# RWKV7 in two blocks of 16: substitution for 16-blocks, the step to 32 on TensorE, and low halves on VectorE

## The chip, the cores and the metric

The kernel runs on one core of one Trainium2 chip. The time is device microseconds of one execution; the metric is the median of the runs. The engines are PE (TensorE), PEld (its weight load), DVE (VectorE), ACT (ScalarE), POOL (GpSimd) and SP (SyncE, which here issues most DMAs). Every engine works off its own list of instructions in order and waits for the others through semaphores.

## The reference

Two transformer blocks on 512 context tokens and further latent ones, width 1024, fp32. The first has a gated linear recurrence and dilated attention, the second a pooling, differential attention, RWKV7 in both directions, and a mixture of experts. The change lies in the RWKV7. Per head it carries a 64x64 state over the tokens, which each token decays, partly erases along one key and updates along another:

```
S_t = S_{t-1} * w_t  +  (S_{t-1} a_t) b_t^T  +  v_t k_t^T
y_t = S_t r_t
```

The kernel takes 64 tokens (a chunk) at once. Within a chunk the erasing terms hang on each other: they are a triangular system (I - A) X = R with a 64x64 strictly triangular A for each head and chunk, whose inverse T is wanted.

## The kernel before

A scheduler decides the order on each engine while the kernel is built, from the program's order and its own estimates; so an engine's list mixes the recurrence with the projections and the attention around it. The weights of projections come in fp32 and are split in `split_chunk` into a high half `wh` (ScalarE, L304) and a low half `wl` (GpSimd, L305), each 128x1024 per piece; a projection is three matmuls into `pf` or `pt` (L310 to L312).

The recurrence goes in 12 batches, two directions taking turns, each of two chunks with eight heads: 16 systems of 64x64, or on 128 partitions. A batch has three parts.

- `ph_a` (from L1128) loads `kb` and `kr` on SP, scans the decays (`cs`, L1142 and L1144), forms `BK` (L1156) and `AR`, multiplies them on TensorE (`pA`, L1162) and writes the masked product to `AMB` (VectorE, L1166); `ptb` (L1171) transposes.
- `ph_i` (L1178) inverts the 32x32 blocks on the diagonal. Four DMAs write them to `atD` in DRAM (L1183) and one reads them back as `LT` (L1186), with each system on a partition, repeated four times, so that each partition has eight of the 32 columns. Then come 31 steps of substitution on VectorE, each a product into `Tm` (L1194) and a sum into `Ti` (L1196), 62 instructions of 28 to 76 elements a partition. Four DMAs write `Ti` to `ttD` (L1199).
- `ph_b` (L1201) runs two batches later. It loads the inverse blocks as `TT` (four DMAs, L1213) and makes the block off the diagonal of the 64x64 inverse with three groups of 16 matmuls of 32x32 into `pi` (L1250, L1255, L1260), each copied out half by VectorE and half by ScalarE (L1245, L1246). Then `px` (L1268), its copy `XV` (L1271, L1272), `pW` (L1282), `WW` (L1289 to L1292), the outputs and the new state `SI` (L1300 to L1312).

`pW` of a batch needs `XV`, and what follows it needs `WW`; both come from VectorE and ScalarE. VectorE's list has these between the steps of another batch's substitution.

Of the kernel before, what the change touches and what calls it, by code (L numbers as in the profile page):

```python
# [39 lines left out]
def _consts():  # L40
    f = np.float32
    groups, off = {g: [] for g in "012345"}, {}
    where = {"bias1": "1", "invf": "1", "cos2": "3", "sin2": "3", "hsel": "5", "hbc": "5",
             "mask": "2", "tinit": "2", "sgn": "2",
             "iota32": "4", "tokid": "4", "tri": "4", "slot": "4", "tokrow": "4"}
# [48 lines left out]
    sg = np.ones((128, 2))  # L94
    for dd, (lt, le) in enumerate(((r[:, None] < r[None, :], r[:, None] <= r[None, :]),
                                   (r[:, None] > r[None, :], r[:, None] >= r[None, :]))):
        tr = np.concatenate([lt, le], 1)
        for e in range(2):
            m[64 * e:64 * e + 64, dd, e] = -0.5 * tr
            m[64 - 64 * e:128 - 64 * e, dd, e] = tr  # L100
    for e in range(2):
        sg[64 * e:64 * e + 64, e] = -0.5
    add("mask", m)
    add("sgn", sg)
    ti = np.zeros((4, 32, 8, 32))
    for g in range(4):
        for q in range(8):
            ti[g, :, q, 4 * q + g] = 1
    add("tinit", ti)
    return {"cst" + g: np.concatenate(v, 1) for g, v in groups.items()}, off  # L110


# [78 lines left out]
def _build(ctx, tc, A, out, dbg, upto):  # L191
# [7 lines left out]
    cur = {}  # L199
# [100 lines left out]
    def split_chunk(raw, name="w"):  # L300
# [1 line left out]
        hi = cur["wp"].tile([128, kt, nw], F32R, tag="hi", name=name + "h", bufs=cur["wb"])  # L302
        lo = cur["wp"].tile([128, kt, nw], F32R, tag="lo", name=name + "l", bufs=cur["wb"])
        SC.activation(hi, raw, AF.Copy)  # L304
        GP.tensor_tensor(lo, raw, hi.bitcast(F32), ALU.subtract)  # L305
        return hi, lo

    def mm3(p, ah, al, bh, bl, start, stop):
# [789 lines left out]
    ones64 = cc("ones")[:, 0:1].to_broadcast([128, 64])
    CW = 0.5 * math.exp(-0.5)
    atD = [dp.tile([2, 2, 8, 32, 32], F32, name="atD%d" % i) for i in range(4)]  # L1100
    ttD = [dp.tile([2, 2, 8, 32, 32], F32, name="ttD%d" % i) for i in range(4)]
    yD = [dp.tile([128, 8, 4, 64], F32, name="yD%d" % d) for d in range(2)]
    par = ((0, E0), (1, E1))
    WWB = 1
    LATB, LPN = 10, (6, 5, 5, 3)

    def w1(name, shape=(4, 64), bufs=1, dt=F32):
# [12 lines left out]
    for d in range(2):  # L1120
        for e in range(2):
# [2 lines left out]
            ir = slice(64, 128) if e == 0 else slice(0, 64)  # L1124
            V.tensor_copy(t[ir], bc(ident[ir, None, ir], [64, 4, 64]))
            SI[d, e] = t

    def ph_a(d, c, s, AMB):  # L1128

# [45 lines left out]
                          AF.Copy, scale=sgn[:, e:e + 1])  # L1175
        return AR, dec

    def ph_i(d, AMB, bi):  # L1178

        for e in range(2):  # L1180
            for i in range(2):
                r0 = 64 * e + 32 * i
                SY.dma_start(atD[bi][e, i].rearrange("q s t -> s q t"),  # L1183
                             AMB[r0:r0 + 32, e, :, :, 32 * i:32 * i + 32].rearrange("p s f t -> p (s f) t"))
        LT = w1("LT", (32, 32), 2)
        SY.dma_start(LT.rearrange("p s t -> p (s t)"),  # L1186
                     atD[bi].rearrange("e i q s t -> (e i q) (s t)")[None].to_broadcast([4, 32, 1024]))
# [9 lines left out]
        td = ttD[bi].rearrange("e i q (j g) t -> g (e i q) j t", g=4)  # L1197
        for g in range(4):
            SY.dma_start(td[g], T[32 * g:32 * g + 32])  # L1199

    def ph_b(d, chs, sts, AMB, bi):  # L1201

        lat, c0 = chs[0] >= 4, min(chs)
        XE, XO = XV1 if lat and d else XV
        T = TT[d]
        fs = [(s, f) for s in range(2) for f in range(4)]
        v3 = vTD[:, c0:c0 + 2].rearrange("t c (f e v) -> e t (c f) v", f=4, e=2)
        SY.dma_start(XE[E1, :, :, 64:128].rearrange("p s f t -> p (s f) t"), v3[0])
        SY.dma_start(XO[E0, :, :, 0:64].rearrange("p s f t -> p (s f) t"), v3[1])
        for e in range(2):  # L1210
            for i in range(2):
                r0 = 64 * e + 32 * i
                SY.dma_start(T[r0:r0 + 32, :, :, 32 * i:32 * i + 32].rearrange("p s f t -> p (s f) t"),  # L1213
                             ttD[bi][e, i].rearrange("q j t -> j q t"))

        def col(p, q, n, o=0):
            return p[:, o + n * q:o + n * (q + 1)]
# [104 lines left out]
    def run_b():  # L1322
        n, sts = pend.pop(0)
        ph_b(*sts)
        if n == 3 and dbg is not None and "S_c" in dbg:
            for d_ in range(2):
                for e, rows in par:
                    SY.dma_start(dbg["S_c"][128 * d_:128 * d_ + 128][rows, 256 * e:256 * e + 256],
                                 SI[d_, e][rows].rearrange("p a b -> p (a b)"))

    def batch(n):
        d, chs = batches[n]
        AMB = w1("AMB", (2, 2, 4, 192), 3)
# [796 lines left out]
```

## Time and profile before

| | |
| --- | --- |
| median of 3 runs | 1983.2 us (1969.72 to 1985.23) |
| the profiled execution | 1981.57 us, span 1979.7 us |
| mean granted TensorE clock over the span | 0.934 |
| PE, PEld busy | 1755.4 us (89%), 1246.3 us (63%) |
| DVE busy | 1091.5 us (55%), 2364 instructions |
| ACT, POOL busy | 619.1 us (31%), 526.5 us (27%) |

The profile is one execution taken by the hardware profiler. The first block ends near 515 us of the span; the twelve batches, with projections between, lie from there to about 1165; differential attention and merges follow, and from about 1474 us on the experts, whose weights fill the DMA queues. The granted clock is that of TensorE as a share of its full speed; matmuls are pipelined, so a busy PE need not be at its peak.

### The profile page before, as it was taken

The numbers are of one execution on the slowest core, as the hardware profiler recorded it, in microseconds if no ns is written. First come the engines' busy times: TensorE is split into PE (matmuls) and PEld (weight loads), VectorE is DVE, ScalarE is ACT, GpSimd is POOL, SyncE is SP. The second block draws the span as 40 slices with busy tenths as digits, with TensorE's granted clock in tenths as the row PEclk, the third lists the DMA queues.
The fourth block names the chain that finished last, engine by engine and source line by source line (L and its number), as shares of the span: only waits on it lengthen the run. The fifth ranks groups of instructions, "written<-read, shape, count | busy, mean of one in ns | idle before, by whom it ended". The sixth has DMA issues, their size and how long they took to land. (4 is left out here: it accounts for less than half of the span.)

```text
span 1979.7 us, 31352 instructions
## 1 busy us (share of the span) xinstructions
PE 1755.4 (89%) x12309; PEld 1246.3 (63%) x12310; DVE 1091.5 (55%) x2364; ACT 619.1 (31%) x1164; POOL 526.5 (27%) x379
## 2 busy tenths in 40 slices
PE   6899998967787887888879998988979999999998
PEld 3874677953565776677667876677954545444544
DVE  4555675275487746777788655776342333332332
ACT  4234454443443222223333233443221111111110
POOL 2510337442335332231331132642310110101010
PEclk8999998988898898889898999999979999999999
DMA  8336513567546445445355338653629999999998
GB/s 298 108 111 218 197 64 103 195 181 250 156 121 171 135 137 122 109 109 137 99 151 152 81 112 280 204 179 111 246 99 387 387 386 386 386 387 386 386 386 289
DMA packets 275295, 415.89 MB, mean 210 GB/s; under 512 B 104876, under 2 KB 126408, under 8 KB 274888
## 3 DMA queue, kind: packets, MB, share of 16 engines
q1 hardware_dynamic: 246248, 383.44, 58.0%
q10 hardware_dynamic: 25568, 16.78, 2.8%
q0 software_dynamic: 3328, 13.63, 2.4%
q8 instruction: 98, 1.61, 0.3%
q14 instruction: 53, 0.43, 0.1%
HBM read 370.26 MB, written 43.53 MB: 209 GB/s over the span
## 5 line engine op out<-in xcount | busy, mean ns | idle before, releaser
L305 POOL TENSOR_TENSOR wl<-wr,wh 128x1024 fp32r<-128x1024 f32 x125 | 308.3, 2473 | 495.8 <-ACT wh L304 455.5
L304 ACT ACTIVATE wh<-wr 128x1024 fp32r<-128x1024 f32 x125 | 131.6, 1054 | 141.2 <-issue 54.9
L1980 POOL TENSOR_TENSOR yl<-ey,yh 128x512 fp32r<-128x512 f32 x30 | 38.4, 1279 | 466.1 <-ACT yh L1979 466.1
L310 PE MATMUL pf<-h2h,wh 128*128 128x512 f32 x344 | 147.8, 430 | 15.6 <-DVE Ti L1196 10.2
L1194 DVE TENSOR_TENSOR Tm<-LT,Ti 128x60 f32<-128x60 f32 (+24 forms) x372 | 116.8, 314 | 76.9 <-DMA LT<-atD 68.2
L311 PE MATMUL pf<-h2l,wh 128*128 128x512 f32 x344 | 144.5, 420 | 0.0
L312 PE MATMUL pf<-h2h,wl 128*128 128x512 f32 x344 | 143.3, 417 | 0.0
L1974 PE MATMUL ped<-wd,hid 128*64 128x512 f32 (+1 forms) x528 | 127.5, 585 | 0.7 <-ACT hid L1958 0.7
L1935 PE MATMUL peg<-wg,hTg 128*64 128x512 f32 x512 | 126.9, 597 | 0.0
L1942 PE MATMUL peu<-wu,hTg 128*64 128x512 f32 x512 | 125.3, 595 | 0.0
L1196 DVE TENSOR_TENSOR Ti<-Ti,Tm 128x60 f32<-128x60 f32 (+24 forms) x372 | 109.3, 294 | 9.1
L2007 DVE TENSOR_TENSOR acc<-acc,pcb 128x512 f32<-128x512 f32 (+1 forms) x124 | 76.0, 665 | 49.1 <-PE pcb L2006 49.0
L310 PEld LDWEIGHTS pf<-h2h,wh 128*128 128x128 f32 x344 | 69.4, 202 | 38.4 <-issue 15.4
L1974 PEld LDWEIGHTS ped<-wd,hid 128*64 128x64 f32 x528 | 39.9, 136 | 70.6 <-issue 65.9
L1942 PEld LDWEIGHTS peu<-wu,hTg 128*64 128x64 f32 x512 | 43.2, 137 | 65.1 <-issue 62.9
L311 PEld LDWEIGHTS pf<-h2l,wh 128*128 128x128 f32 x344 | 68.8, 200 | 18.5 <-issue 3.4
L1935 PEld LDWEIGHTS peg<-wg,hTg 128*64 128x64 f32 x512 | 41.9, 137 | 60.9 <-issue 58.1
L312 PEld LDWEIGHTS pf<-h2h,wl 128*128 128x128 f32 x344 | 68.6, 199 | 18.2 <-issue 2.1
L1282 PE MATMUL pW<-AMB,XV 128*128 128x64 f32 (+1 forms) x256 | 45.2, 335 | 28.7 <-DVE XV L1271 16.9
L1979 ACT ACTIVATE yh<-ey 128x512 fp32r<-128x512 f32 x30 | 18.9, 630 | 163.6 <-DVE ey L1978 90.2
L1915 DVE TENSOR_SCALAR hTg<-pg,gs,sh 128x128 f32<-128x128 f32 x64 | 25.3, 408 | 75.1 <-PE peu L1942 38.4
L1912 ACT ACTIVATE hTg<-pg,sh,gs 128x128 f32<-128x128 f32 x64 | 28.2, 457 | 121.4 <-PE peu L1942 55.4
(961 smaller groups left out, 4475.1 us busy)
## 6 DMA issues: line engine op xcount, KB each, us to landing
wg<-in_w_exp_gate_dram SPq DMA_DIRECT2D x64, 1024.0 KB
wu<-in_w_exp_up_dram SPq DMA_DIRECT2D x64, 1024.0 KB
wd<-in_w_exp_down_dram SPq DMA_DIRECT2D x62, 1024.0 KB
wr<-in_w_in_dram SPq DMA_DIRECT2D x97, 512.0 KB
kb<-kbD SPq DMA_DIRECT2D x24, 384.0 KB
wr<-in_w_out_dram SPq DMA_DIRECT2D x16, 512.0 KB
LT<-atD SPq DMA_DIRECT2D x12, 512.0 KB
thD<-mth ACTq DMA_DIRECT2D x24, 256.0 KB
```

The costliest lines, as they stand in the source:

```text
L304: SC.activation(hi, raw, AF.Copy)
L305: GP.tensor_tensor(lo, raw, hi.bitcast(F32), ALU.subtract)
L310: PE.matmul(p, ah, bh, start=start, stop=False)
L311: PE.matmul(p, ah, bl, start=False, stop=False)
L312: PE.matmul(p, al, bh, start=False, stop=stop)
L1194: V.tensor_tensor(tmp[:, :nj, :n], bc(LT[:, s, None, ts_], [128, nj, n]), bc(T[:, js, s:s + 1], [128, nj, n]), ALU.mult)
L1196: V.tensor_tensor(T[:, js, ts_], T[:, js, ts_], tmp[:, :nj, :n], ALU.add)
L1282: PE.matmul(pw[e][:, nw * f:nw * (f + 1)], X[:, s, f, :], AMB[:, e, s, f, n0:192], start=True, stop=True)
L1935: mm = PE.matmul(pg[64 * a:64 * a + 64, :], hT[:, k, 64 * a:64 * a + 64], gp[a][k // 4][:, k % 4, :], start=(k == 0), stop=(k == 7), tile_ ...
L1942: PE.matmul(pu[64 * a:64 * a + 64, :], hT[:, k, 64 * a:64 * a + 64], up[a][k // 4][:, k % 4, :], start=(k == 0), stop=(k == 7), tile_posit ...
L1974: PE.matmul(pd[64 * a:64 * a + 64, :], hid[:, m * k + 64 * a:m * k + 64 * a + 64], dn[q][a][:, k, 0:q1 - q0], start=(k == 0), stop=(k == 3 ...
L2007: V.tensor_tensor(acc[i][:, qs], acc[i][:, qs], p, ALU.add)
```

## The change

The substitution now inverts 16x16 blocks: `atD` and `ttD` hold blocks of 16, `LT` is 128x256 (128 KB, 512 KB before) and repeated twice, and there are 15 steps (30 instructions). `Ti` is written with two DMAs, and eight read it back into a tile `U` (three buffers), which holds the 16-blocks on the diagonal of each 32-block. A new part `ph_m` joins two blocks of 16 to one of 32, with a batch between: 32 small matmuls transpose `U` (into `tit`, copied to `T16` by ScalarE), 32 multiply with `AMB`, VectorE masks that into `PJ`, 64 more give the joined block and its transpose (`tiu`), and five VectorE sums put them into `TT` and `T16`. With that `ph_b` loses its first group of 16 matmuls and its copy. `WW` gets a second buffer. And in this stage the low halves `wl` of the weights are made on VectorE: 53 of the 125.

```diff
@@ split_chunk
-        GP.tensor_tensor(lo, raw, hi.bitcast(F32), ALU.subtract)
+        cur.get("lo", GP).tensor_tensor(lo, raw, hi.bitcast(F32), ALU.subtract)
@@ the stage
     weights("wp1", 3, "right", 2)
+    cur["lo"] = V
...
-    WWB = 1
+    WWB = 2
@@ ph_i
-            for i in range(2):
-                r0 = 64 * e + 32 * i
+            for i in range(4):
+                r0 = 64 * e + 16 * i
                 SY.dma_start(atD[bi][e, i].rearrange("q s t -> s q t"),
-                             AMB[r0:r0 + 32, e, :, :, 32 * i:32 * i + 32].rearrange("p s f t -> p (s f) t"))
-        LT = w1("LT", (32, 32), 2)
+                             AMB[r0:r0 + 16, e, :, :, 16 * i:16 * i + 16].rearrange("p s f t -> p (s f) t"))
+        LT = w1("LT", (16, 16), 2)
         SY.dma_start(LT.rearrange("p s t -> p (s t)"),
-                     atD[bi].rearrange("e i q s t -> (e i q) (s t)")[None].to_broadcast([4, 32, 1024]))
+                     atD[bi].rearrange("e i q s t -> (e i q) (s t)")[None].to_broadcast([2, 64, 256]))
...
-        for s in (range(31) if d == 0 else range(31, 0, -1)):
+        for s in (range(15) if d == 0 else range(15, 0, -1)):
...
-        for g in range(4):
-            SY.dma_start(td[g], T[32 * g:32 * g + 32])
+        for g in range(2):
+            SY.dma_start(td[g], T[64 * g:64 * g + 64])
+        for e in range(2):
+            for i in range(4):
+                r0, c0 = 64 * e + 16 * i, 16 * (i % 2)
+                SY.dma_start(U[r0:r0 + 16, :, c0:c0 + 16], ttD[bi][e, i].rearrange("q j t -> j q t"))
+    def b32(p, o, lhs, rhs):
+
+        for q in range(8):
+            for e, i, r in blocks:
+                PE.matmul(p[r, o + 32 * q:o + 32 * q + 32], lhs(r, q, e, i), rhs(r, q, e, i), start=True, stop=True,
+                          tile_position=(r.start, r.start))
+
+    def ph_m(d, AMB, U):
...
+        pt = ps("tit", "aux")
+        b32(pt, 0, lambda r, q, e, i: U[r, q], lambda r, q, e, i: eye[r])
+        T = w1("T16", (8, 32), 2)
+        SC.activation(T, q8(pt[:, 0:256]), AF.Copy)
+        b32(pt, 256, at, lambda r, q, e, i: T[r, q])
+        P = w1("PJ", (8, 32))
+        V.tensor_tensor(P, q8(pt[:, 256:512]), bc(join[:, d, None, :], [128, 8, 32]), ALU.mult)
+        pu = ps("tiu", "aux")
+        b32(pu, 0, lambda r, q, e, i: P[r, q], lambda r, q, e, i: U[r, q])
+        b32(pu, 256, lambda r, q, e, i: U[r, q], lambda r, q, e, i: P[r, q])
+        for e, i, r in blocks:
+            V.tensor_tensor(TT[d][r, :, :, 32 * i:32 * i + 32], U[r].rearrange("p (s f) t -> p s f t", s=2),
+                            pu[r, 0:256].rearrange("p (s f t) -> p s f t", s=2, f=4), ALU.add)
+        V.tensor_tensor(T, T, q8(pu[:, 256:512]), ALU.add)
+        return T
@@ ph_b
-        for e in range(2):
-            for i in range(2):
-                r0 = 64 * e + 32 * i
-                SY.dma_start(T[r0:r0 + 32, :, :, 32 * i:32 * i + 32].rearrange("p s f t -> p (s f) t"),
-                             ttD[bi][e, i].rearrange("q j t -> j q t"))
...
-                PE.matmul(col(pi, q, 32)[q1[e]], T[q1[e], s, f, c1], ident[q1[e], q1[e]], start=True, stop=True,
-                          tile_position=(q1[e].start, q1[e].start))
-        evac([T1[q1[e]] for e in range(2)], [sf(pi, q1[e], 0, 32) for e in range(2)])
@@ batch
-        ph_i(d, AMB, n % 4)
-        pend.append((n, (d, chs, sts, AMB, n % 4)))
+        ph_i(d, AMB, U16[n % 3], n % 4)
+        pend.append([n, (d, chs, sts, AMB)])
+        if len(pend) > 1:
+            join_b()
         if len(pend) > 2:
             run_b()
```

What this makes of VectorE's list, around the start of one substitution in the latent part. Before (each row is a line of the kernel, an operation, its output and inputs and the shape):

```order
L1154 TENSOR_TENSOR AR<-kr,ep 128x4x64
L1156 TENSOR_TENSOR BK<-kb,em 128x2x4x64
L1474 TENSOR_TENSOR dql<-dqT,dqh 128x512
L1194 TENSOR_TENSOR Tm<-LT,Ti 128x31
L1271 COPY XV_4514<-px 64x512
L1196 TENSOR_TENSOR Ti<-Ti,Tm 128x31
L1271 COPY XV_4514<-px 64x512
L1194 TENSOR_TENSOR Tm<-LT,Ti 128x30
L1474 TENSOR_TENSOR dql<-dqT,dqh 128x512
L1196 TENSOR_TENSOR Ti<-Ti,Tm 128x30
L1235 COPY AZ<-pta 128x8x64
L1194 TENSOR_TENSOR Tm<-LT,Ti 128x29
```

Of the change, the join (L1244 to L1251) and a low half (L311) ahead of a substitution:

```order
L1244 TENSOR_TENSOR PJ<-tit,cst_4502 128x256
L311 TENSOR_TENSOR wl<-wr,wh 128x1024
L1171 TENSOR_TENSOR BK<-kb,em 128x2x4x64
L1181 TENSOR_TENSOR AMB<-pA,cst_4502 128x4x128 x2
L1157 SCALAR_TENSOR_TENSOR cs<-cst_75,kb 128x64 x4
L1171 TENSOR_TENSOR BK<-kb,em 128x2x4x64
L1249 TENSOR_TENSOR TT_4515<-U_4536,tiu 32x8x32 x4
L1251 TENSOR_TENSOR T_7520<-T_7520,tiu 128x256
L1169 TENSOR_TENSOR AR<-kr,ep 128x4x64
L1159 SCALAR_TENSOR_TENSOR cs<-cst_75,kb 128x64 x2
L1282 COPY AZ<-pta 128x8x64
```

The other work that stood among the steps (XV, AZ) stands ahead of or behind them now, with the join and a low half.

On TensorE, where the small groups stand beside `pW` of another batch. Before:

```order
L1268 MATMUL px<-AZ,TT_4515 64x128 x16
L1227 MATMUL pta<-cst_75,AR 64x64 x11
L1282 MATMUL pW<-AMB,XV_4514 128x128 x4
L1227 MATMUL pta<-cst_75,AR 64x64 x2
L1282 MATMUL pW<-AMB,XV_4518 128x128 x4
L1227 MATMUL pta<-cst_75,AR 64x64 x3
```

Of the change (`tit` with `U` is the first group of the join):

```order
L1227 MATMUL tit<-cst_4502,U_4536 32x32
L1324 MATMUL pW<-AMB,XV_4514 128x64 x4
L1324 MATMUL pW<-AMB,XV_4518 128x64 x4
L1227 MATMUL tit<-cst_4502,U_4536 32x32 x22
L1324 MATMUL pW<-AMB,XV_4514 128x64 x4
L1342 MATMUL pch<-SI_4522,WW 64x64
L1227 MATMUL tit<-cst_4502,U_4536 32x32 x9
L317 MATMUL pf<-h2l_4371,wh 128x512
```

The join's first group, which waits for `U`, stands in pieces before and between the `pW` of the batch before it. In the whole order the 32x32 matmuls of the stage stand in 129 runs; before, in 55.

On SP, from one batch's `atD` writes to the loads of its inverse. Before:

```order
L1183 DMA atD_4506<-AMB 32x8x32 x4
L1186 DMA LT<-atD_4506 128x1x1024
L1132 DMA kb<-kbD_2114 128x768
L297 DMA wr<-in_w_in_dram 128x1024 x2
L1199 DMA ttD_4509<-Ti 256x1x32 x4
L1213 DMA TT_4519<-ttD_4509 32x8x32 x4
L297 DMA wr<-in_w_in_dram 128x1024
```

Of the change:

```order
L1201 DMA atD_4506<-AMB 16x8x16 x8
L1147 DMA kb<-kbD_2114 128x768
L1204 DMA LT<-atD_4506 128x1x256
L303 DMA wr<-in_w_in_dram 128x1024 x3
L1217 DMA ttD_4510<-Ti 512x1x16 x2
L1221 DMA U_4534<-ttD_4510 16x8x16 x8
L1486 DMA boD<-gk_11341 128x512
L303 DMA wr<-in_w_in_dram 128x1024
```

The loads of `U` stand right behind the `ttD` writes whose landing they wait for, and loads of weights stand behind both, as they did before.

## Rows read from the trace of the kernel before

**Rows 1.** Busy us (instructions) per engine by stretch, then granted clock, DMA share, GB/s.

```profile
515.00:780.00 265.00, 224.52 (x1537) 170.34 (x1536) 173.87 (x396) 90.62 (x148) 93.47 (x78) 0.88 0.52 137
780.00:1165.00 385.00, 326.02 (x3702) 280.46 (x3703) 285.83 (x868) 123.48 (x244) 99.16 (x96) 0.89 0.46 119
...
1500.00:1900.00 400.00, 393.76 (x2071) 193.10 (x2068) 132.64 (x250) 54.22 (x104) 32.01 (x25) 1.00 1.05 386
```

**Rows 2.** Waits, 515 to 1165 us: us in total, times, longest us.

```profile
POOL wl L305 <- ACT wh L304: 115.2, 33, 11.8
DVE Tm L1194 <- DMA LT<-atD: 68.2, 10, 11.0
...
PE pW L1282 <- ACT WW L1292: 23.2, 5, 6.5
...
PE pW L1282 <- DVE XV L1271: 16.9, 4, 6.9
...
PE px L1268 <- DVE TT L1245: 15.3, 3, 6.5
...
PE pf L310 <- DVE Ti L1196: 10.2, 2, 8.0
...
PE ptb L1171 <- DVE AMB L1166: 9.0, 5, 4.8
...
PE pi L1250 <- DMA TT<-ttD: 1.3, 2, 0.7
```

**Rows 3.** VectorE's timeline near 975 us: start, us, instruction [idle before <-releaser].

```profile
974.99 0.19 DVE L1194 TENSOR_TENSOR Tm<-LT,Ti 128x31 f32<-128x31 f32 x1 [6.79 <-DMA LT<-atD]
...
978.38 0.42 DVE L1291 TENSOR_TENSOR WW<-pW,AR 64x256 f32<-64x256 f32 x1
```

**Rows 4.** Costliest groups of the page: busy, mean ns of one, idle before.

```profile
L1194 DVE TENSOR_TENSOR Tm<-LT,Ti 128x60 f32<-128x60 f32 (+24 forms) x372 | 116.8, 314 | 76.9 <-DMA LT<-atD 68.2
...
L1196 DVE TENSOR_TENSOR Ti<-Ti,Tm 128x60 f32<-128x60 f32 (+24 forms) x372 | 109.3, 294 | 9.1
```

**Rows 5.** VectorE's groups by shape, 500 to 1190 us; columns as above.

```profile
L1245 DVE COPY TT<-pi 32x256 f32<-32x256 f32 x12 | 5.0, 414 | 1.0 <-PE pi L1260 0.7
...
L1194 DVE TENSOR_TENSOR Tm<-LT,Ti 128x35 f32<-128x35 f32 x12 | 2.3, 196 | 0.3
...
L1194 DVE TENSOR_TENSOR Tm<-LT,Ti 128x16 f32<-128x16 f32 x12 | 2.1, 173 | 0.3
```

**Rows 6.** GpSimd's timeline near 731 us.

```profile
731.71 2.36 POOL L305 TENSOR_TENSOR wl<-wr,wh 128x1024 fp32r<-128x1024 f32 x1 [0.81 <-ACT wh L304]
```

**Rows 7.** VectorE's timeline in the same stretch.

```profile
731.64 0.21 DVE L1194 TENSOR_TENSOR Tm<-LT,Ti 128x50 f32<-128x50 f32 x1
731.89 2.24 DVE L1196 TENSOR_TENSOR Ti<-Ti,Tm 128x50 f32<-128x50 f32 x1
```

**Rows 8.** VectorE's groups by shape, whole span.

```profile
L1073 DVE TENSOR_TENSOR mix<-x,mix 128x1024 f32<-128x1024 f32 x4 | 4.8, 1213 | 0.0
```

**Rows 9.** Waits of SP's queue, 515 to 1165 us; columns as in rows 2.

```profile
SPq L297 <- POOL wl L305: 98.6, 22, 13.7
```

**Rows 10.** SP's timeline, 1084 to 1103 us: one batch's writes and loads being issued.

```profile
1086.43 2.83 SPq L1183 DMA_DIRECT2D atD<-AMB  x4
1090.52 0.58 SPq L1186 DMA_DIRECT2D LT<-atD  x1
1094.61 2.56 SPq L1199 DMA_DIRECT2D ttD<-Ti  x4
1100.58 1.79 SPq L1213 DMA_DIRECT2D TT<-ttD  x4
```

**Rows 11.** VectorE's timeline near 1100 us.

```profile
1099.62 0.19 DVE L1194 TENSOR_TENSOR Tm<-LT,Ti 128x31 f32<-128x31 f32 x1 [5.04 <-DMA LT<-atD]
```

**Rows 12.** A stretch while LT is loaded; columns as in rows 1.

```profile
1092.00:1095.00 3.00, 3.00 (x56) 2.73 (x51) 2.42 (x8) 1.19 (x2) 0.00 (x0) 1.00 0.26 67
```

**Rows 13.** TensorE's timeline near 718 us: a group of 16 small matmuls, 32 records.

```profile
718.43 0.69 PE L1260 MATMUL pi<-TT,Qs 32*32 32x32 f32 x32
```

More of the change, by code (lines that the diff above doesn't have):

```diff
@@ L43, in _consts @@
     where = {"bias1": "1", "invf": "1", "cos2": "3", "sin2": "3", "hsel": "5", "hbc": "5",
-             "mask": "2", "tinit": "2", "sgn": "2",
+             "mask": "2", "tinit": "2", "join": "2", "eye32": "2", "sgn": "2",
              "iota32": "4", "tokid": "4", "tri": "4", "slot": "4", "tokrow": "4"}
@@ L104, in _consts @@
     add("sgn", sg)
-    ti = np.zeros((4, 32, 8, 32))
-    for g in range(4):
+    ti = np.zeros((2, 64, 8, 16))
+    for g in range(2):
         for q in range(8):
-            ti[g, :, q, 4 * q + g] = 1
+            ti[g, :, q, 2 * q + g] = 1
     add("tinit", ti)
+    jn = np.zeros((4, 32, 2, 32))
+    jn[:, 16:, 0, :16] = 1
+    jn[:, :16, 1, 16:] = 1
+    add("join", jn)
+    add("eye32", np.tile(np.eye(32), (4, 1)))
     return {"cst" + g: np.concatenate(v, 1) for g, v in groups.items()}, off
@@ L1099, in _build @@
     CW = 0.5 * math.exp(-0.5)
-    atD = [dp.tile([2, 2, 8, 32, 32], F32, name="atD%d" % i) for i in range(4)]
-    ttD = [dp.tile([2, 2, 8, 32, 32], F32, name="ttD%d" % i) for i in range(4)]
+    join = cc("join").rearrange("p (d j) -> p d j", d=2)
+    eye = cc("eye32")
+    atD = [dp.tile([2, 4, 8, 16, 16], F32, name="atD%d" % i) for i in range(4)]
+    ttD = [dp.tile([2, 4, 8, 16, 16], F32, name="ttD%d" % i) for i in range(4)]
     yD = [dp.tile([128, 8, 4, 64], F32, name="yD%d" % d) for d in range(2)]
     par = ((0, E0), (1, E1))
-    WWB = 1
+    WWB = 2
     LATB, LPN = 10, (6, 5, 5, 3)
@@ L1126, in _build @@
             SI[d, e] = t
+    U16 = []
+    for i in range(3):
+        t = rp.tile([128, 8, 32], F32, name="U16%d" % i)
+        GP.memset(t, 0.0)
+        U16.append(t)
     def ph_a(d, c, s, AMB):
@@ L1176, in ph_a, with ph_i @@
         return AR, dec
-    def ph_i(d, AMB, bi):
+    blocks = [(e, i, slice(64 * e + 32 * i, 64 * e + 32 * i + 32)) for e in range(2) for i in range(2)]
+    fs = [(s, f) for s in range(2) for f in range(4)]
+    def ph_i(d, AMB, U, bi):
         for e in range(2):
-            for i in range(2):
-                r0 = 64 * e + 32 * i
+            for i in range(4):
+                r0 = 64 * e + 16 * i
                 SY.dma_start(atD[bi][e, i].rearrange("q s t -> s q t"),
-                             AMB[r0:r0 + 32, e, :, :, 32 * i:32 * i + 32].rearrange("p s f t -> p (s f) t"))
-        LT = w1("LT", (32, 32), 2)
+                             AMB[r0:r0 + 16, e, :, :, 16 * i:16 * i + 16].rearrange("p s f t -> p (s f) t"))
+        LT = w1("LT", (16, 16), 2)
         SY.dma_start(LT.rearrange("p s t -> p (s t)"),
-                     atD[bi].rearrange("e i q s t -> (e i q) (s t)")[None].to_broadcast([4, 32, 1024]))
-        T = w1("Ti", (8, 32), 2)
+                     atD[bi].rearrange("e i q s t -> (e i q) (s t)")[None].to_broadcast([2, 64, 256]))
+        T = w1("Ti", (8, 16), 2)
         SC.activation(T, tinit, AF.Copy)
-        tmp = w1("Tm", (8, 32))
-        for s in (range(31) if d == 0 else range(31, 0, -1)):
-            js, ts_ = (slice(0, s // 4 + 1), slice(s + 1, 32)) if d == 0 else (slice(s // 4, 8), slice(0, s))
+        tmp = w1("Tm", (8, 16))
+        for s in (range(15) if d == 0 else range(15, 0, -1)):
+            js, ts_ = (slice(0, s // 2 + 1), slice(s + 1, 16)) if d == 0 else (slice(s // 2, 8), slice(0, s))
             nj, n = js.stop - js.start, ts_.stop - ts_.start
@@ L1196, in ph_i, with at, q8, ph_b @@
             V.tensor_tensor(T[:, js, ts_], T[:, js, ts_], tmp[:, :nj, :n], ALU.add)
-        td = ttD[bi].rearrange("e i q (j g) t -> g (e i q) j t", g=4)
-        for g in range(4):
-            SY.dma_start(td[g], T[32 * g:32 * g + 32])
-    def ph_b(d, chs, sts, AMB, bi):
+        td = ttD[bi].rearrange("e i q (j g) t -> g (e i q) j t", g=2)
+        for g in range(2):
+            SY.dma_start(td[g], T[64 * g:64 * g + 64])
[9 more added lines that the diff above has]
+    def ph_m(d, AMB, U):
+        def at(r, q, e, i):
+            return AMB[r, e, fs[q][0], fs[q][1], 32 * i:32 * i + 32]
+        def q8(ap):
+            return ap.rearrange("p (q t) -> p q t", q=8)
+        pt = ps("tit", "aux")
[13 more added lines that the diff above has]
+        return T
+    def ph_b(d, chs, sts, AMB, T1):
         lat, c0 = chs[0] >= 4, min(chs)
@@ L1205, in ph_b @@
         T = TT[d]
-        fs = [(s, f) for s in range(2) for f in range(4)]
         v3 = vTD[:, c0:c0 + 2].rearrange("t c (f e v) -> e t (c f) v", f=4, e=2)
@@ L1239, in ph_b @@
         q2 = [slice(64 * e + 32 - 32 * d, 64 * e + 64 - 32 * d) for e in range(2)]
-        c1, c2 = slice(32 * d, 32 * d + 32), slice(32 - 32 * d, 64 - 32 * d)
+        c2 = slice(32 - 32 * d, 64 - 32 * d)
         pi = ps("pi", "aux")
-        T1, Qs = w1("T1", (2, 4, 32)), w1("Qs", (2, 4, 32))
+        Qs = w1("PJ", (2, 4, 32))
         def evac(dst, src_):
@@ L1249, in ph_b @@
             for e in range(2):
-                PE.matmul(col(pi, q, 32)[q1[e]], T[q1[e], s, f, c1], ident[q1[e], q1[e]], start=True, stop=True,
-                          tile_position=(q1[e].start, q1[e].start))
-        evac([T1[q1[e]] for e in range(2)], [sf(pi, q1[e], 0, 32) for e in range(2)])
-        for q, (s, f) in enumerate(fs):
-            for e in range(2):
-                PE.matmul(col(pi, q, 32)[q2[e]], AMB[q1[e], e, s, f, c2], T1[q1[e], s, f, :], start=True,
+                PE.matmul(col(pi, q, 32)[q2[e]], AMB[q1[e], e, s, f, c2], T1[q1[e], q], start=True,
                           stop=True, tile_position=(q1[e].start, q2[e].start))
@@ L1329, in run_b, with join_b @@
                                  SI[d_, e][rows].rearrange("p a b -> p (a b)"))
+    def join_b():
+        for z in pend:
+            if len(z[1]) == 4 and (len(pend) == 1 or z is not pend[-1]):
+                d, _, _, AMB = z[1]
+                z[1] += (ph_m(d, AMB, U16[z[0] % 3]),)
     def batch(n):
@@ L1384, in _build @@
     while pend:
+        join_b()
         run_b()
@@ L1519, in _build @@
     step(99)
+    cur.pop("lo")
     subpool(None, None)
```

2 lines of the change are left out of this document (1 added, 1 removed).

## Prediction

> **What bounds the kernel now.** I read the busy shares of four stretches first [rows 1]. In the last one, the experts, the DMA share is 1.05 at 386 GB/s and the granted clock 1.00: that stage streams weights, the change does not touch it, and it begins when the stage before it ends. So a microsecond won between 515 and 1165 us, where the twelve batches of the recurrence lie, comes off the whole time. There TensorE is busy 224.52 of 265 and 326.02 of 385 us: idle 40.48 + 58.98 = 99.5 us. [...] VectorE is busy 173.87 + 285.83 = 460 of 650 us. No engine is full; the stage is a chain that goes back and forth.
>
> Next the waits of that stretch [rows 2]. TensorE's large ones are all for products that VectorE makes, or that stand on ScalarE behind one of VectorE: WW 23.2, XV 16.9, TT 15.3, the substitution 10.2, AMB 9.0, together 74.6 of the 99.5 us. VectorE's one large wait is for LT, 68.2 us. The two belong together, since VectorE works in order: in the batch at 975 us the first Tm waits 6.79 us for LT, and the WW that TensorE's pW needs stands behind it [rows 3]. The substitution itself is 116.8 + 109.3 = 226.1 us [rows 4]. Per batch, then, 68.2/12 + 226.1/12 = 5.7 + 18.8 = **24.5 us of VectorE** lie ahead of what TensorE wants.
>
> **VectorE, the substitution.** 744 instructions become 12 x 30 = 360, of 8 to 36 elements a partition. Rows of that size cost 0.173 (16 elements) to 0.196 us (35) [rows 5]: 0.19 each, 68 us, 5.7 per batch. That the 744 average 0.30 has a reason which goes away in part: while GpSimd's subtraction runs from 731.71 for 2.36 us [rows 6], a Ti started at 731.89 takes 2.24 us and ends with it, where the Tm ahead of it took 0.21 [rows 7].
>
> **VectorE, the low halves.** 53 of the 125 move to VectorE. Its nearest row, a two-input 128x1024 operation, takes 1.213 us [rows 8]: 64 us. I take nothing for it on the path, since the rest of VectorE's idle time (650 - 460 = 190 us) can hold it; a bound is all 64. A gain stands against it: SP's weight loads waited 98.6 us for GpSimd's subtraction [rows 9], which frees its buffer after 1.2 instead of 2.4 us. I count neither.
>
> **VectorE, the join.** One product and one sum of 256 columns and four sums 32x256, nearest the 32x256 copies at 0.414 us [rows 5]: 6 x 0.414 = 2.5 us per batch, 30 in all; one such copy goes (5). VectorE's sum over the stage: -226 + 68 + 64 + 30 - 5 = -69 us.
>
> **The loads.** Before, four atD writes take 2.83 us to issue from 1086.43, LT is issued at 1090.52 [rows 10], and the Tm that needs it starts at 1099.62 [rows 11]: 13.2 us, of which 9.1 are LT. Now eight writes are issued: 4 x 2.83/4 = 2.8 us more. LT has a quarter of the bytes; its 9.1 us fall by nothing if they are latency and by 6.8 if all goes with bytes. So from AMB to Tm the change is between +2.8 and -4.0 us. During LT the DMA share is 0.26 [rows 12], about four of 16 engines: the bytes do set much of it, so I take two thirds of 6.8, which is 4.6 shorter and in sum about 2 us shorter: a wait of 3.7 us per batch in place of 5.7 (bounds 1.7 to 8.5).
>
> [...]
>
> **The other round trip.** Before, four ttD writes are issued from 1094.61 and the four TT loads from 1100.58 for 1.79 us [rows 10], and TensorE waited for them 1.3 us in all [rows 2]. Now there are two writes and eight U loads, (8 - 4) x 1.79/4 = 1.8 us more in loads and 2.56/2 = 1.3 less in writes, so the trip is the same. What changes is who stands behind it: the row order has the first product of the join among the pW of the batch before. I count nothing and make it a rival.
>
> **TensorE.** 48 groups of 32 small matmuls come and 12 groups of 16 go. A group of 16 (two records each) takes 0.69 us with two tiles side by side [rows 13]. A new group takes 0.69 if its four tiles run side by side and 1.38 if two do: 33 to 66 us, less 8.3, so 25 to 58. I take 40, about the middle (the order also cuts the groups into more pieces), and 0.85 of it, TensorE's busy share, on the path: 34 us.
>
> [...] By the order the kernel's runs of 32x32 matmuls rise from 55 to 129. [...]
>
> **The sum.** VectorE's block ahead of TensorE falls from 24.5 to 3.7 + 5.7 + 2.5 = 11.9 us, 51% less. I let TensorE's 74.6 us of waiting fall by that share: -38 us (-24 at a wait of 8.5, block 16.7, -32%; -44 at 1.7, block 9.9, -60%). The lower clock follows idleness, in these rows at least: 63 x 38/99.5 = -24 us (0 to -28). TensorE's added work: +34 (21 to 49). Together **-28 us**, between -51 and +25. The profiled execution took 1981.57 us, 1.6 below the median of the runs: 1983.2 - 28 = **1955 us**. The own range of this case is 1935 to 1968.
>
> **Rivals.**
> *VectorE's queue is the bound itself.* Then its whole block counts: 12 x (24.5 - 11.9) = 151 us less, 64 of low halves added, 87 us gained: 1896; with nine batches in twelve it is 1918. For it: VectorE's wait for LT and its busy time are 528 of 650 us. Against: TensorE is at 85% there and gets work added.
> *The U trip takes LT's place.* From the first ttD issue to the last TT issue 7.8 us pass now [rows 10], with other work between on TensorE. The same trip is now ahead of a join of four groups, an evacuation and six VectorE instructions, and only then TT. If TensorE stands 2.5 us more per batch for it, 12 x 2.5 = 30 us go: 1985, no change. For it: the order puts the join's first group early, and the waiting SP queue holds the next weights behind it. Against: 1.3 us of waiting today.
> *TensorE's additions are at their dear end.* 58 x 0.85 = 49 in place of 34, and the clock's return of 24 stays out: 1994, or 1970 with the clock. No change within 1%, mostly.
> *Slower: the low halves hold up VectorE.* GpSimd waited 115.2 us for the high halves [rows 2], where nobody minded. On VectorE such a wait stops the substitution, WW and XV. If half of it moves, 58 us: 1955 + 58 = 2013. It decides for slower from 48 us on, 0.9 us for each of the 53. Against: the order puts each where its high half is planned to be ready; for it: one stands in the middle of a substitution, and plans and chip differ by up to 6.79 us for LT [rows 3].
> *It doesn't do what it says*: excluded for the count of instructions; the order shows 30 rows per batch.
>
> **How the numbers follow.** About 1% (under 1963, over 2003) is what a measurement of this kernel can tell from no change. Chances: the forecast 0.45 (0.39 of it under 1963), VectorE's queue as the bound 0.17, the U trip 0.20 (0.05 still faster, 0.02 slower), TensorE's dear end 0.08 (0.02 faster), the held-up VectorE 0.10 (0.08 slower). Faster: 0.39 + 0.17 + 0.05 + 0.02 = 0.63; slower 0.02 + 0.08 = 0.10; within 1% 0.27. The range goes from 1915, which leaves out about half of the first rival (0.08), to 1992, which leaves out the slower case and a bit (0.11).
>
> **What would show it.** Right: Tm and Ti together near 68 us; VectorE's wait for LT near 45 us; TensorE's waits for WW, XV and TT near half of 55.4; granted clock over 0.90 between 515 and the stage's end; the 32x32 groups about 40 us longer. Wrong: a wait of TensorE or ScalarE for U or the join of over 30 us, a wait of VectorE for the high halves (wl behind wh) of over 30 us, or LT's wait unchanged. The forecast falls if TensorE's waits keep their size under other names.

## The result: 1% slower, with TensorE's added work kept and its waits renamed

The changed kernel takes 2001.0 us (median of 6 runs, 1992.75 to 2008.56), the kernel before 1982.17 (6 runs beside it): a ratio of 1.0105, 95% interval 1.0064 to 1.0146. The forecast was 1955, and 2001 lies outside its range of 1915 to 1992. The profiled execution has a span of 2004.2 us, 24.5 more than before; at 2005.94 us it is 5 us above the change's median, so the stretches below show some 5 us more than the medians do.

The stretch from 500 us to the first matmul of the experts holds the whole difference; columns as in [rows 1]. Before, that matmul starts at 1466.9 us:

```profile
500.00:1466.90 966.90, 825.89 (x6834) 676.75 (x6833) 646.63 (x1573) 334.77 (x616) 309.43 (x252) 0.90 0.51 146
```

and of the change at 1492.1 us:

```profile
500.00:1492.10 992.10, 847.67 (x9517) 702.20 (x9517) 570.21 (x1296) 331.83 (x616) 197.43 (x202) 0.90 0.47 134
```

The stretch is 25.2 us longer. TensorE is busy 21.8 us longer and idle 3.4 us longer (992.1 - 847.7 = 144.4 against 141.0). VectorE has 76.4 us less to do, and GpSimd 112, and none of that reaches the end. The granted clock is 0.90 in both.

The 32x32 groups of TensorE, by line, from 500 to 1215 us (busy, mean ns, idle before). Of the change:

```profile
L1227 PE MATMUL tit<-cst,U 32*32 32x32 f32 x768 | 18.4, 199 | 9.7 <-DMA U<-ttD 9.6
L1227 PE MATMUL tit<-T,AMB 32*32 32x32 f32 x768 | 14.0, 199 | 0.0
L1227 PE MATMUL tiu<-PJ,U 32*32 32x32 f32 x768 | 11.0, 193 | 0.0
L1297 PE MATMUL pi<-T,AMB 32*32 32x32 f32 x384 | 9.9, 204 | 23.9 <-DVE T L1251 23.8
L1227 PE MATMUL tiu<-U,PJ 32*32 32x32 f32 x768 | 9.6, 194 | 1.6 <-DVE PJ L1244 1.6
L1302 PE MATMUL pi<-TT,PJ 32*32 32x32 f32 x384 | 9.5, 205 | 28.2 <-ACT PJ L1293 28.2
```

Of the kernel before:

```profile
L1250 PE MATMUL pi<-cst,TT 32*32 32x32 f32 x384 | 11.0, 195 | 1.3 <-DMA TT<-ttD 1.3
L1255 PE MATMUL pi<-T,AMB 32*32 32x32 f32 x384 | 9.8, 193 | 0.0
L1260 PE MATMUL pi<-TT,Qs 32*32 32x32 f32 x384 | 8.7, 194 | 1.5 <-ACT Qs L1246 1.5
```

They sum to 72.4 us against 29.5: 42.9 more, where 40 were counted. Next to them stand the waits. The waits view of the change, 515 to 1200 us (total, times, longest):

```profile
DVE Tm L1212 <- DMA LT<-atD: 47.8, 11, 11.6
DVE WW L1331 <- PE pW L1324: 47.7, 29, 4.9
DVE wl L311 <- ACT wh L310: 36.0, 20, 4.0
...
PE pi L1302 <- ACT PJ L1293: 28.2, 8, 9.2
...
DVE cs L1157 <- DMA kb<-kbD: 24.5, 9, 7.1
...
PE pi L1297 <- DVE T L1251: 23.8, 7, 8.4
...
DVE cs L1159 <- DMA kb<-kbD: 20.3, 5, 6.6
```

TensorE's five waits of [rows 2], 74.6 us, have shrunk to 9.7 (TT 5.5, AMB 3.3, WW 0.9), with 8.7 more at another product for the substitution, but 28.2 + 23.8 + 9.6 us now stand at the two products `pi` and at `tit`. And VectorE, which waited 68.2 us for LT, waits 47.8 for LT, and 24.5 + 20.3 for `kb`, the load of the next chunk's keys. It also waits 47.7 us for `pW`, where it waited 5.1 before: TensorE and VectorE wait for each other. What that wait costs was not tested.

One batch shows how the two belong together. VectorE's timeline of the change near 975 us:

```profile
974.40 0.42 DVE L1251 TENSOR_TENSOR T<-T,tiu 128x256 f32<-128x256 f32 x1
...
979.59 0.84 DVE L1157 TENSOR_TENSOR_SCAN cs<-cst,kb 128x64 f32<-128x64 f32 x4 [4.17 <-DMA kb<-kbD]
984.28 0.18 DVE L1212 TENSOR_TENSOR Tm<-LT,Ti 128x15 f32<-128x15 f32 x1 [3.85 <-DMA LT<-atD]
...
986.44 0.42 DVE L1292 COPY PJ<-pi 32x256 f32<-32x256 f32 x1
```

TensorE's in the same stretch:

```profile
974.97 0.69 PE L1297 MATMUL pi<-T,AMB 32*32 32x32 f32 x32 [0.70 <-DVE T L1251]
...
987.32 1.06 PE L1302 MATMUL pi<-TT,PJ 32*32 32x32 f32 x32 [9.21 <-ACT PJ L1293]
```

The first `pi` is done by 975.7. Its copy to `PJ` takes 0.42 us on VectorE, but stands there behind a scan that waits 4.17 us for `kb` and a substitution that waits 3.85 us for LT; ScalarE's half of the copy starts only after VectorE's, at 986.89, and TensorE waits 9.21 us. This is the batch at 975 us of [rows 3] over again, with `PJ` in the place of `WW`.

### The profile page after: what moved, and what is told of

Same layout as the page of the kernel before. It is cut to its first block, busy times and chain, and to the rows that moved or that the text cites. A ratio compares the mean times of both kernels' runs of the same rounds, so it can differ in the third digit from the quotient of the medians.

```text
span 2004.2 us, 36551 instructions
## 1 busy us (share of the span) xinstructions
PE 1774.3 (89%) x14997; PEld 1269.0 (63%) x14998; DVE 1015.4 (51%) x2093; ACT 616.7 (31%) x1164; POOL 406.9 (20%) x329
## 5 line engine op out<-in xcount | busy, mean ns | idle before, releaser
L311 POOL TENSOR_TENSOR wl<-wr,wh 128x1024 fp32r<-128x1024 f32 x72 | 182.3, 2541 | 295.8 <-ACT wh L310 292.3
L311 DVE TENSOR_TENSOR wl<-wr,wh 128x1024 fp32r<-128x1024 f32 x53 | 64.8, 1222 | 45.9 <-ACT wh L310 45.6
L2027 PEld LDWEIGHTS ped<-wd,hid 128*64 128x64 f32 x528 | 38.2, 136 | 70.9 <-issue 66.4
L1988 PEld LDWEIGHTS peg<-wg,hTg 128*64 128x64 f32 x512 | 41.4, 137 | 61.9 <-issue 58.6
L317 PEld LDWEIGHTS pf<-h2l,wh 128*128 128x128 f32 x344 | 68.2, 198 | 17.2 <-issue 2.0
L1212 DVE TENSOR_TENSOR Tm<-LT,Ti 128x15 f32<-128x15 f32 (+4 forms) x180 | 34.1, 190 | 52.7 <-DMA LT<-atD 47.8
L316 PE MATMUL pt<-wh,h2h 128*128 128x256 f32 x192 | 60.6, 316 | 0.0
```

Source lines behind the costliest of these rows:

```text
L311: cur.get("lo", GP).tensor_tensor(lo, raw, hi.bitcast(F32), ALU.subtract)
L316: PE.matmul(p, ah, bh, start=start, stop=False)
L317: PE.matmul(p, ah, bl, start=False, stop=False)
L1988: mm = PE.matmul(pg[64 * a:64 * a + 64, :], hT[:, k, 64 * a:64 * a + 64], gp[a][k // 4][:, k % 4, :], start=(k == 0), stop=(k == 7), tile_ ...
L2027: PE.matmul(pd[64 * a:64 * a + 64, :], hid[:, m * k + 64 * a:m * k + 64 * a + 64], dn[q][a][:, k, 0:q1 - q0], start=(k == 0), stop=(k == 3 ...
```

## Experiments

Four theories were tested. A: the added small matmuls make the loss. B: the low halves on VectorE make it. C: VectorE's waits for loads keep TensorE idle as before. D, a part of C: TensorE waits because the copies it needs stand on VectorE behind those loads. Times are medians; each set of four runs had its own runs of the kernel before beside it, from 1978 to 1985 us, and ratios are to those. Where times of two sets are subtracted, the difference is uncertain by a few microseconds for that.

**The low halves, taken back.** The changed kernel with them on GpSimd:

```diff
-    cur["lo"] = V
...
-    cur.pop("lo")
```

> The changed kernel with the low halves back on GpSimd. Theory A (TensorE's added small matmuls set the loss; its waits only changed their names): the time stays within 8 us of 2001. Theory B (the low halves on VectorE, which waited 36 us for the high halves there, hold up TensorE): 1985 or less. Theory C (VectorE waits as long for LT and kb together as before, 98 against 96 us): within 8 us of 2001, with LT and kb again near 90 us.

2005.6 us, ratio 1.0122 (1.0085 to 1.0159). B is out: beside blocks of 16, the low halves on VectorE cost nothing on balance. What VectorE's 36 us of waiting for high halves cost by themselves, a wait that I had named as a sign of a wrong forecast, the run does not say, since the move also spares the substitution 27 us (next experiment). The stretch to the first expert matmul:

```profile
500.00:1487.40 987.40, 849.95 (x9543) 702.24 (x9541) 568.71 (x1249) 333.86 (x619) 313.44 (x255) 0.91 0.47 136
```

C's sign did not come: VectorE waits 39.4 us for LT and 38.2 for `kb` (500 to 1215 us), 77.6 in place of some 90, and yet TensorE is idle 137.4 us. Against the kernel before, VectorE has 129 us less of substitution and waits 21 us less for loads, and TensorE's idle time falls by 3.6. So the loads alone are not what keeps TensorE idle here; its waits at the two `pi` are 39.4 us in this run.

**The low halves alone.** The same lines put into the kernel before:

```diff
-        GP.tensor_tensor(lo, raw, hi.bitcast(F32), ALU.subtract)
+        cur.get("lo", GP).tensor_tensor(lo, raw, hi.bitcast(F32), ALU.subtract)
...
+    cur["lo"] = V
...
+    cur.pop("lo")
```

> The kernel before with only the low halves of this stage moved to VectorE. Theory A: the move costs nothing on TensorE, so 1982 plus or minus 8. Theory B: slower by 15 us or more, 1997 to 2015, with VectorE waiting 30 us or more for high halves. Theory C: as A.

1951.8 us, ratio 0.9834 (0.9795 to 0.9873). None of the theories had this: this part of the change is a gain of some 30 us. The stretch to the first expert matmul:

```profile
500.00:1444.20 944.20, 809.66 (x6857) 668.47 (x6855) 619.14 (x1629) 335.22 (x619) 198.60 (x205) 0.91 0.53 149
```

VectorE's groups of that run, columns as in [rows 4]:

```profile
L1195 DVE TENSOR_TENSOR Tm<-LT,Ti 128x60 f32<-128x60 f32 (+24 forms) x372 | 87.5, 235 | 42.9 <-DMA LT<-atD 34.7
L1197 DVE TENSOR_TENSOR Ti<-Ti,Tm 128x60 f32<-128x60 f32 (+24 forms) x372 | 81.9, 220 | 8.4
L305 DVE TENSOR_TENSOR wl<-wr,wh 128x1024 fp32r<-128x1024 f32 x53 | 65.1, 1229 | 29.8 <-ACT wh L304 29.5
```

The 744 instructions of the substitution take 169.4 us in place of 226.1 [rows 4]: they are no longer held while GpSimd subtracts [rows 6, 7]. In the trace of the kernel before, 35 of the 744 take over 0.5 us, and each of the 35 ends within 0.1 us of the end of a GpSimd instruction, 28 of them of a low half. The end of the holding pays 57 of the 65 us, and the wait for LT is half as long besides (34.7 us for 68.2); SP's weight loads do not wait less (137.5 us behind VectorE, 120.1 behind GpSimd before). How the 30 us divide between the holding and the shorter wait was not tested. With 16-blocks there is less to hold. VectorE's groups of the run with the low halves taken back:

```profile
L1211 DVE TENSOR_TENSOR Tm<-LT,Ti 128x15 f32<-128x15 f32 (+4 forms) x180 | 50.1, 279 | 44.3 <-DMA LT<-atD 39.4
L1213 DVE TENSOR_TENSOR Ti<-Ti,Tm 128x15 f32<-128x15 f32 (+4 forms) x180 | 46.9, 261 | 5.3
```

97.0 us, against 34.1 + 35.7 = 69.8 in the changed kernel: 27 us of holding, not 57. The two parts of the change thus aim in part at the same microseconds. The other part, blocks of 16 with the join, costs 49 us beside low halves on VectorE (1952 to 2001) and 25 beside low halves on GpSimd (1980 to 2006). In the first pair TensorE is busy 38.0 us longer and idle 9.9 us longer: most of the loss is TensorE's added work.

**The join twice.** Each small matmul of it repeated:

```diff
-        for q in range(8):
+        for q in range(16):
+            q = q % 8
             for e, i, r in blocks:
```

> The changed kernel with each small matmul of the join done twice (3072 records more). The small matmuls of the join took about 43 us of TensorE's time. Theory A: 30 to 45 us more, 2031 to 2046. Theories B and C (TensorE waits anyway and the work lies inside its waits): 2001 to 2012.

2052.2 us, ratio 1.0358 (1.0321 to 1.0396), 51 more, 6 above theory A's range. Its stretch from 500 us to the first expert matmul:

```profile
500.00:1533.50 1033.50, 884.28 (x12568) 736.97 (x12566) 566.56 (x1289) 329.27 (x607) 196.05 (x199) 0.90 0.45 129
```

41.4 us longer than the change's, of which TensorE's busy time is 36.6. The join's small matmuls are not hidden here in TensorE's idle time: they come on top, nearly one for one.

**The join in wide matmuls.** One matmul of 256 columns per tile for eight of 32:

```diff
-        for q in range(8):
-            for e, i, r in blocks:
-                PE.matmul(p[r, o + 32 * q:o + 32 * q + 32], lhs(r, q, e, i), rhs(r, q, e, i), start=True, stop=True,
-                          tile_position=(r.start, r.start))
+        for e, i, r in blocks:
+            PE.matmul(p[r, o:o + 256], lhs(r, 0, e, i), rhs(r), start=True, stop=True,
+                      tile_position=(r.start, r.start))
...
```

The four calls pass their operands accordingly.

> The changed kernel with each group of 32 small matmuls of the join as four of 256 columns, one per tile; they take only the first of eight heads as stationary operand, so what is computed in the join is left out in part, while all copies, sums, loads and waits stay. Theory A: TensorE has 25 to 35 us less work and the time falls by 20 to 35 us, to 1966 to 1981. Theories B and C: within 8 us of 2001.

1948.7 us, ratio 0.9838 (0.9797 to 0.9878): 52 less, more than theory A allowed. Its stretch:

```profile
500.00:1425.10 925.10, 824.43 (x6789) 656.96 (x6787) 557.46 (x1288) 328.57 (x608) 195.34 (x199) 0.92 0.49 143
```

TensorE's busy time falls by 23.2 us, its idle time by 43.7 (144.4 to 100.7); the profiled execution, 1939.94 us, is 9 us under its median. The join's four groups still take 46.9 us for 53.0, so most of the gain is not their busy time. The waits, 515 to 1200 us:

```profile
DVE Tm L1212 <- DMA LT<-atD: 42.1, 11, 6.9
...
PE pi L1301 <- ACT PJ L1292: 5.6, 2, 3.1
```

VectorE waits for LT nearly as before, but TensorE waits for `PJ` 5.6 us in place of 28.2, and the wait for the join's last sum, 23.8, is gone. The scheduler, which takes the wide join to be done at another time, wrote VectorE's list in another order. Of the change, around the start of a substitution:

```
L1251 TENSOR_TENSOR T_7956<-T_7956,tiu 128x256
...
L1212 TENSOR_TENSOR Tm<-LT,Ti 128x15
...
L1292 COPY PJ<-pi 32x256
```

With the wide join:

```
L1250 TENSOR_TENSOR T_7368<-T_7368,tiu 128x256
...
L1291 COPY PJ<-pi 32x256
L1212 TENSOR_TENSOR Tm<-LT,Ti 128x15
```

In the last nine substitutions of the change, `PJ` stands behind the first Tm in all nine; with the wide join, ahead of it in six. VectorE's busy time, 557.5 us for 570.2, did not make the difference. The earlier place of `PJ` may have, or the join's shorter chain, four matmuls ahead of each copy in place of 32: this run changes both.

**The copies of pi on ScalarE alone.**

```diff
-            V.tensor_copy(dst[0], src_[0])
-            SC.activation(dst[1], src_[1], AF.Copy)
+            for o, p in zip(dst, src_):
+                SC.activation(o, p, AF.Copy)
```

> The changed kernel with the copies of pi made by ScalarE alone, so that PJ and TT no longer stand on VectorE behind its waits for loads. Theory D (TensorE loses 52 us waiting for PJ and the join's last sum, which stand on VectorE behind its waits for LT and kb; 28 of it for PJ): TensorE's wait for PJ falls from 28 us to under 10, and the time by 15 to 25 us, to 1976 to 1986. Theory A (the added small matmuls occupy TensorE): the wait moves elsewhere, 1993 to 2009.

1994.5 us, ratio 1.0092 (1.0058 to 1.0126). TensorE's waits, 515 to 1200 us:

```profile
PE pi L1297 <- DVE T L1251: 24.4, 10, 5.6
PE dqT L1523 <- DVE gk L1485: 10.7, 2, 5.9
...
PE pi L1302 <- ACT PJ L1293: 5.7, 3, 2.8
```

The wait for `PJ` goes from 28.2 to 5.7 as expected, but the time by 6.5 us only (2.6, if each is taken against its own runs of the kernel before), and the intervals of the two ratios overlap; 24.4 us for the join's last sum stay, and other waits grow (`dqT` for `gk` 4.6 to 10.7). D is right on the wait and wrong on its price: 1994.5 lies outside D's range and within A's.

**One buffer for WW.**

```diff
-    WWB = 2
+    WWB = 1
```

> The changed kernel with one buffer for WW, as before. Its work is the same; only the order that the scheduler writes and the waits for that buffer change. Theories A and D: 1995 to 2010, as the second buffer is no part of either. A difference of more than 10 us either way would say that the written order alone moves the time by as much as the whole change (theory E).

2000.1 us, ratio 1.0136 (1.009 to 1.0183). The second buffer shows no effect, and this one new order did not move the time; that no order could is not shown.

**LT in two loads.**

```diff
-        SY.dma_start(LT.rearrange("p s t -> p (s t)"),
-                     atD[bi].rearrange("e i q s t -> (e i q) (s t)")[None].to_broadcast([2, 64, 256]))
+        for g in range(2):
+            SY.dma_start(LT[64 * g:64 * g + 64].rearrange("p s t -> p (s t)"),
+                         atD[bi].rearrange("e i q s t -> (e i q) (s t)"))
```

> The changed kernel with LT loaded by two DMAs of 64 partitions each in place of one that repeats the data twice. Theory C (VectorE's waits for loads set the loss): the wait for LT falls from 48 us to under 25 and the time by 10 to 25 us, to 1976 to 1991. Theory A: 1995 to 2007. If the DMAs are no faster for it, LT's wait stays over 40 and the run tells nothing of C.

1973.8 us, ratio 0.9973 (0.9949 to 0.9996): 27 less by one load cut in two, 2 more than C allowed. Its waits, 515 to 1200 us:

```profile
DVE Tm L1213 <- DMA LT<-atD: 27.8, 9, 7.3
...
PE pi L1298 <- DVE T L1252: 13.7, 6, 4.2
...
PE pi L1303 <- ACT PJ L1294: 10.4, 5, 4.1
```

LT's wait is 20 us shorter, not quite under 25, and TensorE's two waits at `pi`, which do not touch LT, fall from 52.0 to 24.1 with it, as C and D have it. The waits for `kb` fall too, from 53.1 to 35.3 (500 to 1215 us).

**LT in four loads, in the kernel before**, without and with the low halves on VectorE. The edit, in both:

```diff
-        SY.dma_start(LT.rearrange("p s t -> p (s t)"),
-                     atD[bi].rearrange("e i q s t -> (e i q) (s t)")[None].to_broadcast([4, 32, 1024]))
+        for g in range(4):
+            SY.dma_start(LT[32 * g:32 * g + 32].rearrange("p s t -> p (s t)"),
+                         atD[bi].rearrange("e i q s t -> (e i q) (s t)"))
```

> The kernel before with LT loaded by four DMAs of 32 partitions each, the low halves on GpSimd as before. Theory C (the load of LT is what VectorE, and behind it TensorE, waits for): LT's wait falls from 68 us to under 25 and the time by 30 to 50 us, to 1930 to 1952. If the gain of the split needs the low halves on VectorE too: 1965 to 1985.

> The kernel before with the low halves on VectorE (1952) and LT loaded by four DMAs of 32 partitions each. Theory C: LT's wait falls from 35 us to under 20 and the time to 1930 to 1945. Theory A says nothing on it. If LT's wait is not the limit here: 1946 to 1958.

Alone 1929.8 us, ratio 0.9761 (0.97 to 0.9822); with the low halves 1900.2, ratio 0.9599 (0.9547 to 0.9651), 30 us under the lower end of what was expected. VectorE's wait for LT with the split alone, where it was 68.2:

```profile
DVE Tm L1195 <- DMA LT<-atD: 16.5, 7, 7.2
```

and with both:

```profile
DVE Tm L1196 <- DMA LT<-atD: 11.9, 4, 6.4
```

While the four loads run, in the kernel with both (columns as in rows 1):

```profile
908.50:911.00 2.50, 2.50 (x30) 2.31 (x29) 1.62 (x5) 1.99 (x5) 0.10 (x1) 1.00 0.77 216
```

The DMA share is 0.77 at 216 GB/s, where one load gave 0.26 at 67 [rows 12]. The two gains add, or nearly: 30 for the low halves, 52 for the split. And with loads split in both, blocks of 32 take 1900 and blocks of 16 with their join 1974.

**Both repairs on each side.** The copies on ScalarE and LT split, in the changed kernel; the wide join with LT split; and the copies on ScalarE in the kernel before with low halves and split.

> The changed kernel with both the copies of pi on ScalarE (1994) and LT in two DMAs (1974 alone). Theories C and D together: the two gains add, 1962 to 1970. If they are one gain, because the copies only waited behind LT: 1970 to 1978. In no case under 1950, since TensorE keeps its 30 us of added work (theory A).

> The join in wide matmuls (1949, a part of what it computes left out) with LT in two DMAs. If the wide join gained because its copies now stand ahead of the wait for LT (theory D), little of the split is left to gain: 1938 to 1950. If it gained by TensorE's time alone (theory A), the split's gain of 27 us comes on top: 1915 to 1930.

> The kernel before with low halves on VectorE and LT in four DMAs (1900), with the copies of pi on ScalarE alone besides. Theory D: 10 us or more less, to 1880 to 1890. If VectorE's waits are gone with the split: 1893 to 1908.

The changed kernel comes to 1959.0 us (0.9888, 0.984 to 0.9936): 42 less than the change, more than its two gains together (6.5 + 27) and 3 under the range for that, and still above 1950. The wide join with the split takes 1943.2 (0.9801, 0.9753 to 0.9849), 6 less than without: this wide join has little left to win from a shorter wait, as theory D had it, though LT's wait fell from 42.1 to 17.3 us. The kernel before with all three takes 1887.3 us, ratio 0.9494 (0.9433 to 0.9555), the best here, and beats both kernels by 95 and more. (One of its four runs took 7826 us; nothing in these profiles tells why. The ratio leaves it out, and the median of the other three is 1884.0.) That is 13 less than without the copies, as theory D had it, but the intervals of the two ratios touch. Its stretch to the first expert matmul:

```profile
500.00:1375.90 875.90, 798.62 (x6825) 659.90 (x6822) 612.89 (x1584) 343.03 (x648) 197.56 (x202) 0.93 0.54 160
```

TensorE is idle 77.3 us there, against 141.0 before, and VectorE is busier than in the changed kernel.

## Why the prediction was wrong, step by step

**VectorE's sums were right.** Tm and Ti take 34.1 + 35.7 = 69.8 us (68 foretold), the low halves 64.8 (64), the join's sums and product 30 (30). The steps before had rows of 8 to 76 elements, not of 28 to 76 as the description of the kernel has it; the prediction's prices come from rows of 16 and 35.

**The loads: the wait came out near, in part by luck.** LT's wait is 47.8/12 = 4.0 us per batch (3.7 foretold). SP's timeline of the change shows the price of eight writes:

```profile
970.73 5.01 SPq L1201 DMA_DIRECT2D atD<-AMB  x8
975.83 0.38 SPq L1147 DMA_DIRECT2D kb<-kbD  x1
978.74 0.53 SPq L1204 DMA_DIRECT2D LT<-atD  x1
```

5.0 us in place of 2.8 (twice 2.8 counted), and `kb` is issued behind them. From the issue of LT to the first Tm 5.5 us pass here (984.28), 9.1 in [rows 10, 11]: 3.6 less, where 4.6 were taken. From the first `atD` write to Tm the time is not shorter at all, 13.6 us against 13.2, where I had some 2 less. VectorE's wait for LT is shorter all the same, in this batch because VectorE has by then already stood waiting 4.17 us for `kb`. While LT is loaded (columns as in rows 1):

```profile
1122.00:1126.00 4.00, 0.32 (x3) 0.12 (x1) 0.00 (x0) 0.00 (x0) 0.00 (x0) 0.81 0.12 33
```

a DMA share of 0.12 at 33 GB/s, where it was 0.26 at 67 before [rows 12]. At these rates 128 KB take 4.0 us and 512 KB 7.8, an estimate: half the time for a quarter of the bytes. My value had the bytes' time fall to a quarter; with half, 0.67 x 9.1/2 = 3.0 us would have stood for the 4.6, nearer to the 3.6. What I missed is `kb`: I had SP's queue in view for U and not for it. The waits for it over the whole stage, before (500 to 1190 us):

```profile
DVE cs L1144 <- DMA kb<-kbD: 17.4, 5, 7.0
DVE cs L1142 <- DMA kb<-kbD: 13.2, 7, 4.3
```

and of the change (500 to 1215 us):

```profile
DVE cs L1159 <- DMA kb<-kbD: 28.6, 7, 6.6
DVE cs L1157 <- DMA kb<-kbD: 24.5, 9, 7.1
```

30.6 us have become 53.1. With LT, VectorE waits 98.8 us for loads before and 100.9 now: what LT gave, `kb` took. Not all of it comes from the added DMAs: with the low halves alone, which add none, the waits for `kb` are 48.0 us (500 to 1215 us), and with the blocks of 16 alone 38.2. Why `kb` comes later was not tested alone.

**TensorE's work was right, and its weight about right.** 42.9 us more in small groups (40 counted), 21.8 us more busy in all (34 counted on the path); with the low halves on VectorE on both sides it is 38.0, on GpSimd on both sides 24.1. The join done twice shows that this work is paid in full (36.6 us more busy, 41.4 us longer).

**The step that failed** is "I let TensorE's 74.6 us of waiting fall by that share", and the clock's 24 us that hung on it. No run shows the 63 us from which those 24 are worked out; what the runs showed is the granted clock from 500 us to the first expert matmul, between 0.90 and 0.93 in all of them: 0.90 with 141.0 us of TensorE's idle time before, 0.93 with 77.3 in the best run here. The share, 51%, came from the length of VectorE's block. In the batch near 975 us TensorE waits not for the block's length but for one product that stands in VectorE's order behind loads that have not come: a 0.42 us copy behind 8 us of waiting. VectorE's waits for loads lasted as long as before in sum, and the join gave TensorE two new products to wait for. The waits that the prediction named did fall, by more than half, but new ones took their place: TensorE's idle time was 144.4 us for 141.0, and the clock stayed at 0.90. Without these two terms the same sum is +34 against a measured +21.8 + 3.4 = +25.2 in the profile, 18.8 by the medians. That the loads set much of this idle time is shown by the cut loads, which won 27 us here and 52 in the kernel before; that they set all of it is not: with the low halves back on GpSimd the loads' waits were 21 us shorter and the time no better. How much is the join's own chain stays open. The prediction named the sign of it: the forecast falls "if TensorE's waits keep their size under other names".

**The rivals.** "VectorE's queue is the bound itself" is wrong: it lost 76 us of work and the end came later. The U trip itself costs TensorE 9.6 us; with the join's last sum, which that rival put behind it, 33.4, near its 30, and a wait of over 30 us for U or the join was named as a sign of being wrong. The low halves hold VectorE up for 36 us, and taking them back changes nothing: that rival counted the wait and not the 27 us of holding that go with the move. "TensorE's additions at their dear end" is closest, 1994 without the clock's return: its end of 58 was too dear, but the waits that it let shrink did not. What no rival had is that half of this change, the low halves, is worth 30 us alone, where I counted neither a cost nor a gain: the 57 us of holding stood in the prediction as a detail and not as a price.

## What to carry to other kernels

Ask of every wait what ends it. If it ends with a load, try the load before the work of the waiting engine: here one DMA that repeats its data over partitions, cut into four, gave 52 us where the new algorithm lost 25 to 49. And in an in-order list look for the short copies that stand behind such a wait: a copy of 0.42 us kept TensorE waiting for 9.21. But price such a wait by a run, since the time fell by only 6.5 us when it was taken away. Two edits that remove in part the same loss do not add, so run them apart before they go in together.

## What the runs showed of the hardware

A load of 512 KB that repeats 128 KB four times over the partitions ran at a DMA share of 0.26 (67 GB/s), and as four loads of 32 partitions at 0.77 (216 GB/s), in kernels that differ by edit in nothing else but the low halves; what other DMAs moved in these stretches is in both shares. And the 744 two-input instructions of the substitution on VectorE took 169.4 us where they had taken 226.1, 57 less, a quarter of their time, when GpSimd's subtractions did not run beside them.
